# Four small moves in a one-core hybrid decoder layer: first weights on SyncE's queue, a decay subtraction on VectorE, a head's last transposes a step later, a last store in two

## The chip, the cores and the metric

The kernel runs on one core of a Trainium2 chip. The metric is device time in microseconds of one execution of the whole program. The engines are named as in the profile: PE is TensorE (matmuls), PEld its weight loads, DVE is VectorE, ACT is ScalarE, POOL is GpSimd and SP is SyncE, which here only issues DMAs. A letter q behind an engine's name means its own issuing of DMAs or semaphores.

## The reference

One decoder layer on 1024 tokens of width 1024, all in float32:

```python
h = rmsnorm(x, pre_g)
z = einsum('bsd,de->bse', h, w_in)       # one combined input projection
a_u, a_v, a_gate, b_q, b_k, b_v, b_gate, b_lr = split(z)
# branch A: gated unit over chunks of 128 tokens, 8 channel groups
a_out = chunked_sgu(gelu(a_u), gelu(a_v), ...) * silu(a_gate)
# branch B: gated linear attention, 4 heads, dk = 128, dv = 256, chunks of 64 tokens
log_a = log_sigmoid(b_lr @ w_a2 + b_a2) / 16
b     = cumsum(log_a, within a chunk)
qe, ke   = q * exp(b - b_ref), k * exp(b_ref - b)       # b_ref: b in the middle of the chunk
o_intra  = causal(qe @ ke.T) @ v
chunk_kv = (k * exp(b_last - b)).T @ v                  # b_last: b at the chunk's end
o_inter  = (q * exp(b)) @ state       # state = decay * state + chunk_kv, chunk by chunk
b_out = rmsnorm_per_head(o_intra + o_inter) * silu(b_gate)
y = concat(a_out, b_out) @ w_out                        # one output projection
out = x + rmsnorm(y, post_g)
```

Four exponentials are made of `b`: exp(b - b_ref), exp(b_ref - b), exp(b) and exp(b_last - b). The change touches the last one's argument.

## The kernel before

**Matmuls.** Every float32 matrix is held as a high part (a rounded copy that TensorE takes at full rate) and a low part (the rest). `split` (L108, L109) makes them: ScalarE casts the high part, VectorE (or GpSimd, where named) subtracts to get the low one. `mm3` (L114 to L116) then spends three matmuls on each product. A tile of 512 columns over the 1024 input channels is 8 times 3 = 24 matmuls.

**Start.** The 1024 tokens are 8 tiles of 128. `prep` (L267) takes one tile of x, computes its norm, scales it to `h` (L283, two halves) and transposes h on TensorE into `hT`, four transposes to a half, each half split into parts. The first tile's x comes in two halves on SyncE's queue (L263). `block_a` (L128) loads the weights of a block of 512 columns in four pieces of 256 channels, each piece as two DMAs of 256 KB (L135), and splits them into `gr`. In the first block (pieces `raw_125` to `raw_128` in the lists below) the first piece goes out on ScalarE's queue and the others on SyncE's. `first_block` (L209) multiplies a token tile with this block.

**The heads.** For each of four heads `gates` (L394) is run for each half of the tokens: it forms the logarithm of the decay (ScalarE: Abs, Exp, Ln), m (L408, L413), the running sum b by a scan (L415), `d` = b - b_ref (L420, VectorE) and `f` = b_last - b (L424, GpSimd), and the four exponentials on ScalarE: ke (L428), d (L429), b (L430), f (L431). ScalarE loads a table ahead of Exp after another function. `qk` (L441) multiplies them with the projections of q and k (ke L448, ks L449 to L451, d L454, m and b L455 to L457). For heads 2 and 3 the first half's gates are run ahead, during the head before. `attend` (L480) does one token tile: scores times values, the state `st` (L499), and the sums of squares and products of `og` (L513, L516). Every second token tile, GpSimd makes the reciprocal root and VectorE scales `og` (L520). These rows are transposed on TensorE (L527), copied by ScalarE (L528), and after four tiles written to DRAM as `mix_d` by a DMA of GpSimd (L534).

**What sets the order.** A small list of work for later: `later(fn, n)` (L75) puts a function down, and `tick()` (L78), which is called after every 12 matmuls of a projection, runs those that have come due at their n-th tick. So n says how many pieces of projection stand between. Beside this, a scheduler orders the instructions of each engine by its own model, unless `tc.issue_after` binds one behind another; so an edit in one place can move instructions of others. `gr` has 4 buffers, the raw weights 3, PSUM 8 banks.

**Beside the heads** sixteen units (L217 to L240) load blocks of the output weights, form four sums on VectorE (L230, 128x256 each), split them and store them; their DMAs are on SyncE's queue.

**After the heads** come the values and gates of branch A (L574 to L799): Gelu (L656), sums of hT (L609, L613) and their parts, statistics. Then the output projection, as seven products of blocks (`product`, L895). The last product's `done` (L979) squares and sums a token tile's result, and `finish` (L937) makes the root on GpSimd, scales and adds the residual (L942) and stores (L946), in the pieces it is given, on SyncE's and ScalarE's queue in turn. C0 and C1 are the first and the second 512 columns.

Of the kernel before, what the change touches and what calls it, by code (L numbers as in the profile page):

```python
# [11 lines left out]
AF = mybir.ActivationFunctionType  # L12
ALU = mybir.AluOpType
PSUM = bass.MemoryType.PSUM

P = 128
S = 1024
D = 1024
NT = S // P
# [5 lines left out]
CH = 64  # L25
TAU = 16.0
# [7 lines left out]
def hybrid_layer(  # L34
# [16 lines left out]
    nc = tc.nc  # L51
    x, out = x[0], out[0]
# [22 lines left out]
    def later(fn, n=1):  # L75
        pending.append([n, fn])
# [41 lines left out]
    W = 512  # L118
# [9 lines left out]
    def block_a(cols, raws=None, issued=None, behind={}):  # L128

        got = []  # L130
        for k2 in range(KT // 2):
            raw = raws[k2] if raws else raw_tile([2, W])
            c = 0
            for c0, n in cols:
                load = (nc.scalar if raws and k2 == 0 else nc.sync).dma_start(  # L135
                    raw[:, :, c : c + n],
                    w_in[k2 * 256 : (k2 + 1) * 256, c0 : c0 + n].rearrange("(k p) c -> p k c", p=P),
                )
                if issued is not None:
                    issued.append(load)  # L140
                c += n
            hi, lo = granule([2, W])
            if raws:
                for j in range(2):
                    with ExitStack() as order:
                        for made in behind.get(k2, ()):
                            order.enter_context(tc.issue_after(made.ins))
                        split(hi[:, j], lo[:, j], raw[:, j])
            else:
                split(hi, lo, raw)  # L150
            got += [(hi[:, j], lo[:, j]) for j in range(2)]
        return got
# [181 lines left out]
    with tc.tile_pool(name="gla", bufs=1) as gp:  # L334
# [3 lines left out]
            out=causal, in_=causal, pattern=[[1, P]], base=0, channel_multiplier=-1,  # L338
# [11 lines left out]
        for i in range(4):  # L350
# [4 lines left out]
            out=w2[32:64], in0=w2_raw[32:64], in1=w2[32:64].bitcast(F32), op=ALU.subtract  # L355
# [8 lines left out]
        for r, w in enumerate(w_lr):  # L364
            nc.gpsimd.memset(w.bitcast(F32), 0.0)
            src = lr_raw[:, 4 * r : 4 * r + 4]
            for i in (0, 1, 3):
                nc.scalar.copy(out=w[:, :, 32 * i : 32 * i + RANK], in_=src)
            nc.gpsimd.tensor_tensor(
                out=w[:, :, 64 : 64 + RANK], in0=src, in1=w[:, :, 0:RANK].bitcast(F32), op=ALU.subtract  # L370
# [23 lines left out]
        def gates(hd, hf):  # L394

            pz = bank()
            nc.tensor.matmul(
                pz, w2[:, hd * DK : (hd + 1) * DK], lrT[:, hf * 512 : (hf + 1) * 512],
                start=True, stop=True,
            )  # L400
            bias = ba[:, hd : hd + 1]

            f = gp.tile([P, 8, CH], F32, tag="f", name="f")
            sp = f.rearrange("p n c -> p (n c)")
            nc.scalar.activation(out=sp, in_=pz, func=AF.Abs, bias=bias)
            m = gp.tile([P, 8, CH], F32, tag="m", name="m")
            mf = m.rearrange("p n c -> p (n c)")
            nc.vector.tensor_scalar(  # L408
                out=mf, in0=pz, scalar1=bias, scalar2=0.0, op0=ALU.add, op1=ALU.min
            )  # L410
            nc.scalar.activation(out=sp, in_=sp, func=AF.Exp, scale=-1.0)
            nc.scalar.activation(out=sp, in_=sp, func=AF.Ln, bias=1.0)
            tt(out=mf, in0=mf, in1=sp, op=ALU.subtract)  # L413
            b = gp.tile([P, 8, CH], F32, tag="b", name="b")
            nc.vector.tensor_tensor_scan(  # L415
                out=b.rearrange("p n c -> p (n c)"), data0=seg, data1=mf, initial=0.0,
                op0=ALU.mult, op1=ALU.add,
            )
            d = gp.tile([P, 8, CH], F32, tag="d", name="d")
            tt(  # L420
                out=d, in0=b, in1=b[:, :, CH // 2 - 1 : CH // 2].to_broadcast([P, 8, CH]),
                op=ALU.subtract,
            )
            nc.gpsimd.tensor_tensor(  # L424
                out=f, in0=b[:, :, CH - 1 : CH].to_broadcast([P, 8, CH]), in1=b, op=ALU.subtract
            )
            ke = gp.tile([P, 8, CH], F32, tag="ke", name="ke")
            nc.scalar.activation(out=ke, in_=d, func=AF.Exp, scale=-1.0 / TAU)  # L428
            nc.scalar.activation(out=d, in_=d, func=AF.Exp, scale=1.0 / TAU)  # L429
            nc.scalar.activation(out=b, in_=b, func=AF.Exp, scale=1.0 / TAU)  # L430
            nc.scalar.activation(out=f, in_=f, func=AF.Exp, scale=1.0 / TAU)  # L431
            dec = gp.tile([P, LINE, 1], F32, tag="dec", name="dec", bufs=2)[:, 0:8]
            nc.vector.tensor_copy(dec, b[:, :, CH - 1 : CH])
            dec2 = gp.tile([P, LINE, 1], F32, tag="dec2", name="dec2", bufs=3)[:, 0:4]
            tt(out=dec2, in0=dec[:, 0::2], in1=dec[:, 1::2], op=ALU.mult)
            return b, d, f, ke, dec, dec2, m
# [48 lines left out]
        def attend(hd, t, got, v, sg, cur):  # L485
# [31 lines left out]
            if e == 1:  # L517
                rsqrt(oss, oss)
                for i in range(2):
                    nc.vector.tensor_scalar_mul(og[:, i], og[:, i], oss[:, i : i + 1])  # L520

                def out(t=t, og=og, mx=cur["mx"], hd=hd):
                    pt = bank()
                    ptv = pt.rearrange("p (e t c) -> p e t c", t=2, e=2)
                    for i in range(2):
                        for k in range(2):
                            nc.tensor.transpose(ptv[:, k, i], og[:, i, k * P : (k + 1) * P], ident)  # L527
                    nc.scalar.copy(  # L528
                        out=mx[:, :, (t - 1) * P : (t + 1) * P],
                        in_=pt.rearrange("p (e n) -> p e n", e=2),  # L530
                    )
                    if t % 4 == 3:
                        c = slice((t - 3) * P, (t + 1) * P)
                        nc.gpsimd.dma_start(  # L534
                            mix_d[2 * hd : 2 * hd + 2, :, c].rearrange("e p c -> p e c"), mx[:, :, c]
                        )

                later(out, 4 if t == NT - 1 else 3)

        def new_mix():  # L540
            return {"mx": slot_b([P, 2, S])}
# [273 lines left out]
    with tc.tile_pool(name="outp", bufs=1, side="right", reuse_waits="tile") as op:  # L815
# [121 lines left out]
        def finish(hf, t, xr, pieces):  # L937
            r = slice((4 * hf + t) * P, (4 * hf + t + 1) * P)
            rstd = small[:, 16 + 4 * hf + t : 17 + 4 * hf + t]
            rsqrt(rstd, ss[hf][t][:, 0:1], ss[hf][t][:, 1:2])  # L940
            for i, c in enumerate(pieces):
                nc.vector.scalar_tensor_tensor(  # L942
                    out=y[hf][t][:, c], in0=y[hf][t][:, c], scalar=rstd, in1=xr[:, c],
                    op0=ALU.mult, op1=ALU.add,
                )
                (nc.sync, nc.scalar)[i % 2].dma_start(out[r, c], y[hf][t][:, c])  # L946
# [32 lines left out]
        def done(t):  # L979
            sum_sq(ss[1][t][:, 0:1], u[t])  # L980
            vtt(out=y[1][t][:, C0], in0=u[t], in1=pog[:, C0], op=ALU.mult)
            finish(1, t, xrs[t], (C1, C0))

        product(u, "a22", "-t4", False, done)

# [24 lines left out]
```

## Time and profile before

| what | value |
|---|---|
| time, median of 3 runs | 776.02 us (773.84 to 777.74) |
| the profiled execution | 775.63 us |
| its span, first to last instruction | 773.9 us |
| TensorE busy | 753.5 us, 97% |
| VectorE busy | 499.8 us, 65% |
| ScalarE busy | 389.3 us, 50% |
| GpSimd busy | 131.2 us, 17% |
| mean granted TensorE clock | 0.999 |

The profile is of one execution. Busy time is the union of an engine's instructions, not a sign that it sets the time; the waits and the idle time in brackets, with what ended it, tell who was late. TensorE's instructions overlap, so a matmul's own duration is longer than the distance from one start to the next.

### The profile page before, as it was taken

Reading aid. Unit: us, or ns where it says so; the run is one execution under the profiler, and the core shown is the slowest. Engines: PE = TensorE matmul, PEld = TensorE weight load, DVE = VectorE, ACT = ScalarE, POOL = GpSimd, SP = SyncE. Lnnn points to the kernel's source line nnn. Section 1 sums busy time; section 2 is a strip of 40 time slices with the busy share of each in tenths; the row PEclk is TensorE's granted clock in tenths of the full one; section 3 lists DMA queues with packets and bytes.
Section 4 is the critical chain, followed back from the end, with each engine's and each line's share of the span. In section 5 each row is a group of like instructions: output and inputs, shape, how many; then the busy total and the mean of one; then the engine's idle time right before and its main releaser. Section 6 shows DMA issues by size and latency. Waiting matters only on the chain.

```text
span 773.9 us, 10106 instructions
## 1 busy us (share of the span) xinstructions
PE 753.5 (97%) x3680; PEld 622.8 (80%) x3680; DVE 499.8 (65%) x865; ACT 389.3 (50%) x680; POOL 131.2 (17%) x173
## 2 busy tenths in 40 slices
PE   6999999999999999999999999999999999999996
PEld 3787788787888888888878888888888788888885
DVE  4756689856666575654897289565565587534665
ACT  5635567637364746434442237556655652434431
POOL 2225144422222222322100000000000100000043
PEclk9999999999999999999999999999999999999999
DMA  9545520243622462343121012111211696346157
GB/s 293 182 135 177 170 76 1 83 177 121 199 82 83 154 220 72 107 162 112 57 80 28 0 55 55 55 54 55 55 54 55 206 356 226 109 164 244 56 217 272
DMA packets 79412, 97.87 MB, mean 126 GB/s; under 512 B 5569, under 2 KB 62913, under 8 KB 79362
## 3 DMA queue, kind: packets, MB, share of 16 engines
q1 hardware_dynamic: 75760, 87.64, 34.4%
q0 software_dynamic: 2480, 8.01, 3.3%
q10 hardware_dynamic: 1122, 1.58, 0.6%
q8 instruction: 29, 0.48, 0.3%
q14 instruction: 21, 0.17, 0.1%
HBM read 72.04 MB, written 25.17 MB: 126 GB/s over the span
## 4 chain that ended last, share of the span: by engine, by line
PE 74%; DVE 8%; DMA 6%; ACT 6%; issue 2%; POOL 1%; SPq 1%; DVEq 0%; POOLq 0%; ACTq 0%
PE ps L114 24%; PE ps L116 24%; PE ps L115 23%; DMA wb<-in_w_out_dram 3%; DMA wo_d<-wb 3%; PE ps L702 2%; DVE wb L230 1%; DVE wb L109 1%; DMA raw<-in_w_in_dram 1%; POOL f L424 1%; SPq L227 1%; ACT wh L108 1%; PE ps L527 1%; DVE og L520 1%; DVE stl L109 1%
## 5 line engine op out<-in xcount | busy, mean ns | idle before, releaser
L114 PE MATMUL ps<-gr,hT 128*128 128x512 f32 x384 | 152.3, 399 | 5.0 <-ACT hT L108 3.9
L116 PE MATMUL ps<-gr,hT 128*128 128x512 f32 x384 | 150.4, 393 | 0.0
L115 PE MATMUL ps<-gr,hT 128*128 128x512 f32 x384 | 150.2, 393 | 0.0
L109 DVE TENSOR_TENSOR gr<-raw,gr 128x1024 fp32r<-128x1024 f32 (+1 forms) x97 | 91.2, 961 | 22.9 <-ACT gr L108 22.3
L114 PE MATMUL ps<-hT,gr 128*128 128x512 f32 x256 | 100.3, 394 | 0.7 <-ACT u L775 0.7
L115 PE MATMUL ps<-hT,gr 128*128 128x512 f32 x256 | 100.0, 391 | 0.0
L116 PE MATMUL ps<-hT,gr 128*128 128x512 f32 x256 | 99.1, 393 | 0.0
L108 ACT CAST gr<-raw 128x1024 fp32r<-128x1024 f32 (+1 forms) x97 | 78.9, 838 | 36.8 <-PE ps L116 18.3
L114 PEld LDWEIGHTS ps<-gr,hT 128*128 128x128 f32 x384 | 72.8, 190 | 20.3 <-ACT hT L108 4.5
L116 PEld LDWEIGHTS ps<-gr,hT 128*128 128x128 f32 x384 | 72.7, 189 | 15.5 <-DVE hT L109 0.9
L114 PE MATMUL ps<-gr,ah 128*128 128x512 f32 x216 | 84.0, 389 | 0.0
L115 PE MATMUL ps<-gr,ah 128*128 128x512 f32 x216 | 84.0, 389 | 0.0
L115 PEld LDWEIGHTS ps<-gr,hT 128*128 128x128 f32 x384 | 72.8, 190 | 13.8
L116 PE MATMUL ps<-gr,al 128*128 128x512 f32 x216 | 81.4, 389 | 0.0
L114 PEld LDWEIGHTS ps<-hT,gr 128*128 128x128 f32 x256 | 48.1, 188 | 10.3 <-ACT u L775 1.2
L116 PEld LDWEIGHTS ps<-hT,gr 128*128 128x128 f32 x256 | 48.1, 188 | 10.2 <-DVE gr L109 0.2
L115 PEld LDWEIGHTS ps<-hT,gr 128*128 128x128 f32 x256 | 48.1, 188 | 9.6
L230 DVE TENSOR_TENSOR wb<-wb 128x256 f32<-128x256 f32 x64 | 28.8, 450 | 39.7 <-DMA wb<-in_w_out_dram 38.9
L115 PEld LDWEIGHTS ps<-gr,ah 128*128 128x128 f32 x216 | 40.5, 188 | 8.5
L114 PEld LDWEIGHTS ps<-gr,ah 128*128 128x128 f32 x216 | 40.5, 188 | 8.5
L116 PEld LDWEIGHTS ps<-gr,al 128*128 128x128 f32 x216 | 40.5, 188 | 8.3
L108 ACT CAST ah<-a 128x512 fp32r<-128x512 f32 x38 | 23.3, 622 | 46.7 <-PE ps L115 44.9
(232 smaller groups left out, 1323.5 us busy)
## 6 DMA issues: line engine op xcount, KB each, us to landing
raw<-in_w_in_dram SPq DMA_DIRECT2D x78, 256.0 KB, 3.2
gr<-wo_d SPq DMA_DIRECT2D x16, 1024.0 KB, 4.8
wb<-in_w_out_dram SPq DMA_DIRECT2D x64, 128.0 KB, 2.5
wo_d<-wh SPq DMA_DIRECT2D x16, 512.0 KB, 2.8
wo_d<-wb SPq DMA_DIRECT2D x16, 512.0 KB, 2.9
raw<-in_w_out_dram SPq DMA_DIRECT2D x12, 512.0 KB, 3.9
mix_d<-mixB POOLq DMA_DIRECT2D x8, 512.0 KB, 3.1
raw<-in_w_in_dram SPq DMA_DIRECT2D x8, 512.0 KB, 3.7
```

What stands on the lines that cost most here:

```text
L108: cast = nc.scalar.copy(out=hi, in_=src)
L109: return cast, (eng or nc.vector).tensor_tensor(out=lo, in0=src, in1=hi.bitcast(F32), op=ALU.subtract)
L114: nc.tensor.matmul(ps, a[0], b[0], start=start, stop=False, **how)
L115: nc.tensor.matmul(ps, a[0], b[1], start=False, stop=False, **how)
L116: nc.tensor.matmul(ps, a[1], b[0], start=False, stop=stop, **how)
L227: nc.sync.dma_start(b[:, i], w_out[(row + j) * P : (row + j + 1) * P, c : c + 256])
L230: sub = lambda out, a, c: nc.vector.tensor_tensor(out=out, in0=a, in1=c, op=ALU.subtract)
L424: nc.gpsimd.tensor_tensor(out=f, in0=b[:, :, CH - 1 : CH].to_broadcast([P, 8, CH]), in1=b, op=ALU.subtract)
L520: nc.vector.tensor_scalar_mul(og[:, i], og[:, i], oss[:, i : i + 1])
L527: nc.tensor.transpose(ptv[:, k, i], og[:, i, k * P : (k + 1) * P], ident)
L702: nc.tensor.matmul(pt[:, c], part[:, c], wsT[:, g], start=True, stop=True)
```

## The change

Four edits. The first block's first piece of weights is loaded by SyncE like the others. The subtraction `f` is made by VectorE, and the exponentials are written as ke first, and f, d and b bound to stand behind it. The transposes of a head's last two token tiles come due at the fifth tick and not at the fourth; the others stay at the third. The last piece of the last token tile (its first 512 columns) is scaled and stored as two pieces of 256.

```diff
--- before.py
+++ after.py
@@ -132,7 +132,7 @@
             raw = raws[k2] if raws else raw_tile([2, W])
             c = 0
             for c0, n in cols:
-                load = (nc.scalar if raws and k2 == 0 else nc.sync).dma_start(
+                load = nc.sync.dma_start(
                     raw[:, :, c : c + n],
                     w_in[k2 * 256 : (k2 + 1) * 256, c0 : c0 + n].rearrange("(k p) c -> p k c", p=P),
                 )
@@ -421,14 +421,13 @@
                 out=d, in0=b, in1=b[:, :, CH // 2 - 1 : CH // 2].to_broadcast([P, 8, CH]),
                 op=ALU.subtract,
             )
-            nc.gpsimd.tensor_tensor(
-                out=f, in0=b[:, :, CH - 1 : CH].to_broadcast([P, 8, CH]), in1=b, op=ALU.subtract
-            )
+            tt(out=f, in0=b[:, :, CH - 1 : CH].to_broadcast([P, 8, CH]), in1=b, op=ALU.subtract)
             ke = gp.tile([P, 8, CH], F32, tag="ke", name="ke")
-            nc.scalar.activation(out=ke, in_=d, func=AF.Exp, scale=-1.0 / TAU)
-            nc.scalar.activation(out=d, in_=d, func=AF.Exp, scale=1.0 / TAU)
-            nc.scalar.activation(out=b, in_=b, func=AF.Exp, scale=1.0 / TAU)
-            nc.scalar.activation(out=f, in_=f, func=AF.Exp, scale=1.0 / TAU)
+            first = nc.scalar.activation(out=ke, in_=d, func=AF.Exp, scale=-1.0 / TAU)
+            with tc.issue_after(first.ins):
+                nc.scalar.activation(out=f, in_=f, func=AF.Exp, scale=1.0 / TAU)
+                nc.scalar.activation(out=d, in_=d, func=AF.Exp, scale=1.0 / TAU)
+                nc.scalar.activation(out=b, in_=b, func=AF.Exp, scale=1.0 / TAU)
             dec = gp.tile([P, LINE, 1], F32, tag="dec", name="dec", bufs=2)[:, 0:8]
             nc.vector.tensor_copy(dec, b[:, :, CH - 1 : CH])
             dec2 = gp.tile([P, LINE, 1], F32, tag="dec2", name="dec2", bufs=3)[:, 0:4]
@@ -535,7 +534,7 @@
                             mix_d[2 * hd : 2 * hd + 2, :, c].rearrange("e p c -> p e c"), mx[:, :, c]
                         )
 
-                later(out, 4 if t == NT - 1 else 3)
+                later(out, 5 if t == NT - 1 else 3)
 
         def new_mix():
             return {"mx": slot_b([P, 2, S])}
@@ -979,7 +978,7 @@
         def done(t):
             sum_sq(ss[1][t][:, 0:1], u[t])
             vtt(out=y[1][t][:, C0], in0=u[t], in1=pog[:, C0], op=ALU.mult)
-            finish(1, t, xrs[t], (C1, C0))
+            finish(1, t, xrs[t], (C1, C0) if t < 3 else (C1, slice(0, W // 2), slice(W // 2, W)))
 
         product(u, "a22", "-t4", False, done)
```

(`t == NT - 1` is the last token tile of a head. In the lists of the changed kernel the lines behind 424 are one less than before: L520 becomes L519, L528 becomes L527, and so on; the exponentials stand at L426 ke, L428 f, L429 d, L430 b.)

VectorE at the start of the program, before. `raw_125` to `raw_128` are the first block's weights, `h` the normed first token tile:

```order
L283 SCALAR_TENSOR_TENSOR h<-xt,ss,ps 128x512 x2
L109 TENSOR_TENSOR gr<-raw_125,gr 128x512 x2
L109 TENSOR_TENSOR hT<-ps,hT 128x4x128
L109 TENSOR_TENSOR gr<-raw_126,gr 128x512 x2
L109 TENSOR_TENSOR hT<-ps,hT 128x4x128
```

And after:

```order
L283 SCALAR_TENSOR_TENSOR h<-xt,ss,ps 128x512
L109 TENSOR_TENSOR gr<-raw_125,gr 128x512 x2
L283 SCALAR_TENSOR_TENSOR h<-xt,ss,ps 128x512
L109 TENSOR_TENSOR hT<-ps,hT 128x4x128
L109 TENSOR_TENSOR gr<-raw_126,gr 128x512 x2
L109 TENSOR_TENSOR hT<-ps,hT 128x4x128
```

The second half of h moved behind the low parts of the first weights.

ScalarE in the second gates of head 1, before. L412 is the logarithm, `gr` are weights, `mixB` the copy of transposed rows:

```order
L412 ACTIVATE f<-f 128x512
L108 CAST gr<-raw 128x1024
L108 CAST sth<-st 128x256
L513 ACTIVATE og,oss<-ps 128x256
L528 COPY mixB<-ps 128x2x256
L431 ACT_TABLE_LOAD
L431 ACTIVATE f<-f 128x512
L428 ACTIVATE ke<-d 128x512
L430 ACTIVATE b<-b 128x512
L108 CAST gr<-raw 128x1024
L429 ACTIVATE d<-d 128x512
```

And after:

```order
L412 ACTIVATE f<-f 128x512
L108 CAST sch<-scm 128x512
L108 CAST gr<-raw 128x1024
L108 CAST sth<-st 128x256
L512 ACTIVATE og,oss<-ps 128x256
L527 COPY mixB<-ps 128x2x256
L108 CAST gr<-raw 128x1024
L426 ACT_TABLE_LOAD
L426 ACTIVATE ke<-d 128x512
L428 ACTIVATE f<-f 128x512
L430 ACTIVATE b<-b 128x512
L429 ACTIVATE d<-d 128x512
```

The second cast of weights moved ahead of the table load and the exponentials; f's exponential moved from the first to the second place.

VectorE in head 1, where the first gates of head 2 are run ahead, before. `m` (L408) is the first instruction of these gates on VectorE, `wb` are sums of output weights:

```order
L408 TENSOR_SCALAR m<-ps,ba 128x512
L499 SCALAR_TENSOR_TENSOR st<-st,dec_949,ps 128x256
L230 TENSOR_TENSOR wb<-wb 128x256
L413 TENSOR_TENSOR m<-m,f 128x512
L230 TENSOR_TENSOR wb<-wb 128x256
L516 TENSOR_TENSOR og<-ps,sg 128x256
L109 TENSOR_TENSOR stl<-st,sth 128x256
L415 SCALAR_TENSOR_TENSOR b<-seg,m 128x512
L230 TENSOR_TENSOR wb<-wb 128x256
L520 TENSOR_SCALAR og<-og,oss 128x256 x2
L499 SCALAR_TENSOR_TENSOR st<-st,dec_1161,ps 128x256
L420 TENSOR_TENSOR d<-b 128x512
```

And after:

```order
L515 TENSOR_TENSOR og<-ps,sg 128x256
L109 TENSOR_TENSOR stl<-st,sth 128x256
L109 TENSOR_TENSOR vl<-ps,vh 128x256
L519 TENSOR_SCALAR og<-og,oss 128x256 x2
L408 TENSOR_SCALAR m<-ps,ba 128x512
L230 TENSOR_TENSOR wb<-wb 128x256
L413 TENSOR_TENSOR m<-m,f 128x512
L230 TENSOR_TENSOR wb<-wb 128x256
L415 SCALAR_TENSOR_TENSOR b<-seg,m 128x512
L230 TENSOR_TENSOR wb<-wb 128x256
L420 TENSOR_TENSOR d<-b 128x512
L424 TENSOR_TENSOR f<-b 128x512
```

The two scalings of `og` moved ahead of the gates' first instruction, one update of the state ahead of this stretch, and f's subtraction (L424) is new behind d's.

## Rows read from the trace of the kernel before

**Rows 1.** The page: TensorE's busy us (share), instructions; granted clock by slice.

```profile
PE 753.5 (97%) x3680; PEld 622.8 (80%) x3680; DVE 499.8 (65%) x865; ACT 389.3 (50%) x680; POOL 131.2 (17%) x173
PEclk9999999999999999999999999999999999999999
```

**Rows 2.** TensorE's waits and what for: us in total, times, longest.

```profile
PE ps L114 <- ACT hT L108: 3.9, 2, 3.6
PE ps L527 <- DVE og L520: 1.8, 1, 1.8
PE ps L114 <- ACT gr L108: 1.1, 1, 1.1
PE ps L466 <- DVE d L454: 0.8, 1, 0.8
PE ps L114 <- ACT vh L108: 0.5, 1, 0.5
PE ps L468 <- DVE b L456: 0.4, 1, 0.4
```

**Rows 3.** Timeline, first 13 us: start, us, engine, line, operation [idle before].

```profile
1.35 0.42 ACTq L135 DMA_DIRECT2D raw<-in_w_in_dram  x1
3.45 0.38 ACTq L135 DMA_DIRECT2D raw<-in_w_in_dram  x1
6.39 1.41 DVE L283 SCALAR_TENSOR_TENSOR h<-xt,ss,ps 128x512 f32<-128x512 f32 x2 [5.31 <-POOL ss L103]
7.20 1.97 PE L290 MATMUL ps<-ident,h 128*128 128x128 f32 x8 [1.00 <-DVE h L283]
11.14 1.14 ACT L108 CAST gr<-raw 128x512 fp32r<-128x512 f32 x2 [5.84 <-DMA raw<-in_w_in_dram]
12.81 0.80 PE L114 MATMUL ps<-gr,hT 128*128 128x512 f32 x1 [3.65 <-ACT hT L108]
```

**Rows 4.** DMA issues at 1.35 and 3.45: KB, us to landing.

```profile
raw<-in_w_in_dram ACTq DMA_DIRECT2D x1, 256.0 KB, 4.8
raw<-in_w_in_dram ACTq DMA_DIRECT2D x1, 256.0 KB, 7.6
```

**Rows 5.** A stretch: busy (x) of five engines, clock, DMA share, GB/s.

```profile
10.00:11.00 1.00, 0.00 (x0) 0.00 (x0) 0.00 (x0) 0.00 (x0) 0.00 (x0) 1.00 1.12 355
```

**Rows 6.** Lines 424 and 420: ns min/median/max; who waited (us, times).

```profile
L424 POOL TENSOR_TENSOR f<-b x8: 1043/1746/2785, 82.4 to 303.2; 128x512 f32<-128x512 f32 x8
...
  ACT f L431: 9.1, 5
...
L420 DVE TENSOR_TENSOR d<-b x8: 679/1034/1529, 82.3 to 304.1; 128x512 f32<-128x512 f32 x8
```

**Rows 7.** Timeline of ScalarE and GpSimd, second gates of head 1.

```profile
137.95 2.79 POOL L424 TENSOR_TENSOR f<-b 128x512 f32<-128x512 f32 x1 [3.31 <-ACT mixB L528]
137.95 1.28 ACT L431 ACT_TABLE_LOAD   x1
142.34 1.03 ACT L108 CAST gr<-raw 128x1024 fp32r<-128x1024 f32 x1
```

**Rows 8.** Timeline of VectorE, first gates of head 2, within head 1.

```profile
180.43 1.40 DVE L520 TENSOR_SCALAR og<-og,oss 128x256 f32<-128x256 f32 x2
```

**Rows 9.** Timeline of VectorE and ScalarE after the last head.

```profile
370.75 2.50 DVE L609 TENSOR_TENSOR u<-hT 128x512 f32<-128x512 f32 x4 [5.69 <-PE ps L527]
377.55 1.28 ACT L656 ACT_TABLE_LOAD   x1 [0.51 <-DMA mix_d<-mixB]
408.22 1.21 DVE L109 TENSOR_TENSOR gr<-raw,gr 128x1024 fp32r<-128x1024 f32 x1
```

**Rows 10.** The end: timeline, a DMA issue, and 128x256 steps (busy, mean ns).

```profile
769.44 1.41 DVE L942 SCALAR_TENSOR_TENSOR y<-y,small,xr 128x512 f32<-128x512 f32 x2 [0.36 <-POOL small L103]
...
out_dram<-y ACTq DMA_DIRECT2D x2, 256.0 KB, 2.0
...
L230 DVE TENSOR_TENSOR wb<-wb 128x256 f32<-128x256 f32 x64 | 28.8, 450 | 39.7 <-DMA wb<-in_w_out_dram 38.9
```

## The prediction

> **What bounds the kernel now.** I read the page's busy times and slices first: TensorE is busy 753.5 of the span's 773.9 us, at a granted clock of 9 tenths or more in every slice [rows 1]. So the time is TensorE's instruction list plus its pauses, some 20 us, and an edit pays only where TensorE waits. The second view is TensorE's waits by what ended them [rows 2]: they are short and each has its own place. The largest, 3.9 us for hT, is nearly all at the start. Then come 1.8 us for `og` (the rows that a head's transposes read), 1.1 us for a cast `gr` (weights), 0.8 us for `d`, 0.5 for `vh`, 0.4 for `b`. The change can win only part of this, so the scale is a few microseconds, under 1%. I then looked at each place in the timeline, and last at the tail.
>
> **First weights.** Before, the first block's first two loads (256 KB each) go out on ScalarE's queue, at 1.35 and 3.45 us. They take 4.8 and 7.6 us to land [rows 4], so the first is there at 6.1 and the second at 11.05. ScalarE's casts wait 5.84 us for the latter and start at 11.14; hT's cast stands behind them, and the first matmul starts at 12.81 after 3.65 us of idleness [rows 3]. In that stretch the DMA engines are full (share 1.12 at 355 GB/s [rows 5]), so moving a load to another queue moves no byte faster; it changes whose bytes come first. After the change the two loads stand directly behind the two halves of x on SyncE, ahead of six loads that used to go in parallel. Landing T has the bounds 6.1 (where the first one was) and 11.05 (where the second was). I take T = 7.9: both loads one behind the other take 1.5 us at 355 GB/s, which put behind the 6.1 gives 7.6, and 0.3 for x, which shares the stretch.
> The order also changes on VectorE: the second half of h now stands behind both lo parts of these weights. From T on: two casts 1.14 us, the second lo 0.7 behind them (a subtraction of this shape takes 0.68 [rows 6]), half of h 0.7 (1.41 for two), four of the eight transposes about 1.0 (1.97 for eight) [rows 3], and some 0.2 of handing over: T + 3.7 = 11.6 for the first matmul, against 12.81: -1.2. At T = 7.0 the gain is 2.1; at 9.1 it is gone; at 11.05 it is a loss of 1.9; T = 6.1 would give 3.0. The first block's 24 matmuls then run as before.
> The second load's 7.6 us for 256 KB, 35 GB/s, is about a tenth of what the engines moved at 355 [rows 4, 5]. The Trainium skill ("DMA: Bandwidth & Descriptors", "Queues, rings and completion order") says that each DMA engine goes round the queues that have work, a packet at a time. By that, ScalarE's queue would have had half of the rate beside SyncE's alone, its second load would have been there before 8, and leaving its queue would win nothing: this term 0, the sum -2.15. The trace's tenth does not agree with a half, so I keep -1.2.
>
> **The decays' subtraction.** Eight instructions `f` leave GpSimd (median 1.75 us, 1.04 to 2.79) and become 128x512 subtractions on VectorE, like L420, whose fastest is 0.68: 8 x 0.69 = 5.5 us more work. Against it, L420 itself takes 1.03 in the median and 1.53 at worst, beside GpSimd's `f`; all eight at the fastest give back about 8 x (1.03 - 0.68) = 2.8. VectorE's net is under 3 us over 220 us in which it is far from full. ScalarE no longer waits 9.1 us for `f` [rows 6], and `ke` comes first of the four exponentials. What that is worth, place by place:
> Head 1's second gates. ScalarE loaded the table at 137.95, waited for GpSimd's 2.79 us `f`, and the cast `gr`, queued behind f, ke and b, started at 142.34 [rows 7]; TensorE stood 1.1 us for it [rows 2]. In the new order this cast stands ahead of the table load. At 142.34 it has no wait of its own, so no row shows its weights late; it would be done by 139.2, some 4 us early: -1.1. If something else is late there, 0.
> Head 2's first gates, run ahead within head 1. The scalings `og` stood on VectorE behind the scan and all that the scan waits for, at 180.43 [rows 8]; TensorE's transposes waited 1.8 [rows 2]. In the new order they stand ahead of the gate's first instruction: -1.8. Late next is `vh`, whose cast on ScalarE now stands behind ke, f, b and d together; where head 3's gates, run ahead in head 2, make such a queue, TensorE waits 0.5 for it [rows 2], so +0.5 here. Net -1.3 (bounds -1.8 and 0). That 0.5 itself loses GpSimd's part of its delay: -0.3 (-0.5 to 0).
> Cost: in the gates that a head runs for itself, `b` was the second exponential and is now the third or fourth, one exponential (0.63 or a little less) later, and the ks products come ahead of it on VectorE. Its product already is the last to come at one place, 0.4 us [rows 2]; there b slips by up to 1.2 while waits for ks go: +0.4 (0 to +1.2). The 0.8 for `d` stays. Elsewhere the cover is TensorE's projection matmuls, which do not need the decays; were it gone everywhere, rival D.
>
> **A head's last transposes.** `later` 5 instead of 4 sets them one projection piece, 12 matmuls, later: at 753.5 / 3680 = 0.2 us each [rows 1] about 2.5 us. TensorE does the same work, and none of its waits is there; in the first three heads only the copy and the DMA to `mix_d` stand behind them, which is read after the heads, so nothing. After the last head this moves: VectorE waited 5.69 us for these transposes and began its sums at 370.75, and ScalarE's table for GELU waited for the mix DMA until 377.55 [rows 9]. Both go 2.5 later. VectorE then works almost without a pause to the lo part at 408.22 [rows 9], which makes weights that TensorE takes soon after: little room. The new order has three 128x512 steps fewer ahead of that part, 1.9 us at 2.50 / 4 each. What passes through is 0 to 1.0; I take +0.3.
>
> **Last piece of the last token tile.** Two 128x512 steps (1.41 together) from 769.44 and a DMA of 2.0 us end the span. A 128x256 form takes 0.45 [rows 10], so two are 0.2 longer than one of 0.7, but the first goes out 0.25 earlier and both DMAs carry half the bytes, worth up to 0.4 of the 2.0: -0.15 (-0.35 to +0.3).
>
> **Sum.** -1.2 - 1.1 - 1.3 - 0.3 + 0.4 + 0.3 - 0.15 = -3.35. The profiled execution took 775.63 (span 773.9 and 1.7 around it), so 772.3; from the runs' median, 776.02, it is 772.7. I take 772.5.
>
> **Rivals.** 0.5% is 3.9 us, about what a measurement of this kernel can tell from no change: faster means under 772.1, slower over 779.9.
> A, the forecast: chance 0.48. Its own range is 770.9 to 774.0; 0.22 of it lies under 772.1.
> B, the start gains nothing: the engines are full there, T is 9 or later. For it: the share of 1.12 [rows 5], and that h now waits behind the lo parts. Against: the tenth of the rate that the second load had. -3.35 + 1.2 = -2.15: 773.6 from the point I took, 773 to 775.5 with T up to 11.05; chance 0.24, all of it the same.
> C, more is won: T = 7.0 (0.9 more), no new wait for vh (0.5) and b's product in time (0.4): -5.15, 770.7, or 769.6 with T = 6.1 and the edit at the last head free. For it: ScalarE is rid of 9.1 us of waits. Against: its queue then has four exponentials in a row. Chance 0.20, all faster.
> D, VectorE becomes the bound of the gates: `f` (0.69) stands in line ahead of the products, and f's exponential (0.5) ahead of b and d: 1.2 for each of eight gates, 9.6 us where nothing hides it. -3.35 + 9.6 = +6.25: 782. It makes the kernel slower from three gates of the eight (3.35 / 1.2) and passes the 0.5% from about six. For it: b's product is the last to come at one place. Against: TensorE's waits for d and b are 1.2 us together now [rows 2]. Chance 0.08, half of it over 779.9.
> The chances: faster 0.22 + 0.20 = 0.42, same 0.26 + 0.24 + 0.04 = 0.54, slower 0.04. The range goes from C's far end, 769.6, to 776.0, just over B's, and leaves out D and a little of C.
>
> **What would show it.** The first matmul near 11.6 and ScalarE's first cast near 7.9; the waits for `gr` L108 and `og` gone from TensorE's list; L420's eight all near 0.69; a new wait for `vh` near 183 and one for `b` near 126 of 0.4 to 1.6; the sums of the last stage's start 2.5 later and nothing new on TensorE from 370 to 412. It is wrong if the first cast still waits beyond 9, if waits for ke, ks or b appear in several gates, or if TensorE waits for lo parts of `gr` near 410.

## The result and the profile after

The changed kernel takes 770.10 us (median of 4 runs, 768.47 to 770.72) against 775.65 us of the kernel before (4 runs, 773.84 to 777.74): a ratio of 0.9937, with a 95% interval from 0.9919 to 0.9955, or 5.5 us less. Its profiled execution took 769.79 us, with a span of 768.1 us; the span of before was 773.9, so the two traces differ by 5.8 us. Each of them is of one execution. One execution of the experiments below, the traced one of the first edit alone, took 1950.67 us with its matmuls 0.62 us apart, and no number below is taken from it.

TensorE's waits in the changed kernel (what waited, for what, total, times, longest, in us):

```profile
PE ps L290 <- DVE h L283: 4.0, 2, 3.3
...
PE ps L114 <- ACT hT L108: 0.8, 1, 0.8
...
PE ps L475 <- DVE ks L450: 0.7, 1, 0.7
...
PE ps L526 <- DVE og L519: 0.3, 1, 0.3
PE ps L114 <- ACT vh L108: 0.2, 1, 0.2
```

Against [rows 2], the wait for `gr` L108 (1.1) is gone, that for `og` is 0.3 instead of 1.8 (and at the next pair of tiles, near 190; at the old place there is none), that for `vh` 0.2 instead of 0.5, and those for `d` (0.8) and `b` (0.4) are gone too; a wait for `ks` of 0.7 is new. At the start the wait has only changed its name: 3.3 us for `h` where 3.6 stood for hT.

Compared matmul by matmul, TensorE in the changed kernel is ahead of the kernel before by 1.0 us near 39 us, 2.5 near 112, 3.6 near 151, 5.1 near 200 and 6.0 near 312, and by 5.9 from 360 us on. These are the places of the start, of the pause for `d` and `b`, of the one for `gr`, of the one for `og`, and of several small ones.

The start, in the timeline of the changed kernel (start, us, engine, line, operation):

```profile
1.70 5.42 SPq L135 DMA_DIRECT2D raw<-in_w_in_dram  x8
...
8.57 1.14 ACT L108 CAST gr<-raw 128x512 fp32r<-128x512 f32 x2 [3.61 <-DMA raw<-in_w_in_dram]
9.22 1.29 DVE L109 TENSOR_TENSOR gr<-raw,gr 128x512 fp32r<-128x512 f32 x2 [2.42 <-ACT gr L108]
...
10.43 0.74 DVE L283 SCALAR_TENSOR_TENSOR h<-xt,ss,ps 128x512 f32<-128x512 f32 x1
...
11.23 1.11 PE L290 MATMUL ps<-ident,h 128*128 128x128 f32 x4 [3.25 <-DVE h L283]
...
11.99 0.77 PE L114 MATMUL ps<-gr,hT 128*128 128x512 f32 x1
```

The casts start at 8.57 instead of 11.14 [rows 3], 2.6 us earlier, but the first matmul at 11.99 instead of 12.81, only 0.8 earlier: between them stand the two lo parts, then the half of h (10.43), then its four transposes (11.23), as the new order on VectorE has it. The start differs from execution to execution, so one pair of traces is thin evidence. Over the experiments below, the first casts start between 8.57 and 9.41 in the four traces with the first edit and no other change at the start, and between 10.71 and 11.62 in the five without it; the 24th matmul of the first block starts between 19.00 and 19.57, against 19.75 to 20.82.

Lines 420 and 424 in the changed kernel (ns min/median/max), and the scalings of `og` (L519, before L520):

```profile
L420 DVE TENSOR_TENSOR d<-b x8: 678/682/692, 81.3 to 298.3; 128x512 f32<-128x512 f32 x8
...
L424 DVE TENSOR_TENSOR f<-b x8: 676/684/686, 81.9 to 298.9; 128x512 f32<-128x512 f32 x8
...
L519 DVE TENSOR_SCALAR og<-og,oss x32: 341/349/355, 111.5 to 358.8; 128x256 f32<-128x256 f32 x32
```

All eight of L420 take 0.68 now; its median was 1.03 and its worst 1.53 [rows 6]. No scaling takes more than 0.36; before, the two at 180.43 took 1.40 [rows 8].

The second gates of head 1 on ScalarE, in the changed kernel:

```profile
134.30 1.05 ACT L108 CAST gr<-raw 128x1024 fp32r<-128x1024 f32 x1
135.37 1.28 ACT L426 ACT_TABLE_LOAD   x1
137.06 0.63 ACT L426 ACTIVATE ke<-d 128x512 f32<-128x512 f32 x1 [0.40 <-DVE d L420]
```

The cast `gr` is ahead of the table load, where [rows 7] had it 4.4 us behind; ke waits 0.40 for `d` and nothing waits for `f`.

After the last head, VectorE and, by its waits from 360 to 410 us, TensorE (for which that view lists nothing):

```profile
367.61 2.50 DVE L608 TENSOR_TENSOR u<-hT 128x512 f32<-128x512 f32 x4 [8.41 <-PE ps L526]
...
402.88 1.22 DVE L109 TENSOR_TENSOR gr<-raw,gr 128x1024 fp32r<-128x1024 f32 x1
```

The sums start 3.1 us earlier than before [rows 9], in a stretch in which everything else is 5.9 earlier, so 2.7 later: 12 matmuls, 0.23 us apart, as the third edit should have it. TensorE does not notice.

### The profile page after: what moved, and what is told of

It is laid out like the page before. It is cut to its first block, busy times and chain, and to the rows that moved or that the text cites. A ratio compares the mean times of both kernels' runs of the same rounds, so it can differ in the third digit from the quotient of the medians.

```text
span 768.1 us, 10129 instructions
## 1 busy us (share of the span) xinstructions
PE 751.9 (98%) x3680; PEld 622.6 (81%) x3680; DVE 497.9 (65%) x874; ACT 390.0 (51%) x680; POOL 118.8 (15%) x165
## 4 chain that ended last, share of the span: by engine, by line
PE 84%; DMA 4%; ACT 4%; DVE 4%; issue 2%; POOL 1%; SPq 1%; POOLq 0%; DVEq 0%; ACTq 0%
PE ps L114 26%; PE ps L115 26%; PE ps L116 26%; DMA wo_d<-wb 2%; PE ps L701 2%; DMA wb<-in_w_out_dram 2%; PE ps L381 1%; DMA raw<-in_w_in_dram 1%; DVE wb L230 1%; PE ps L475 1%; PE ps L526 1%; DVE wb L109 1%; ACT wh L108 1%; PE ps L465 0%; PE ps L467 0%
## 5 line engine op out<-in xcount | busy, mean ns | idle before, releaser
L108 ACT CAST gr<-raw 128x1024 fp32r<-128x1024 f32 (+1 forms) x97 | 78.8, 838 | 36.1 <-PE ps L116 19.3
L108 ACT CAST ah<-a 128x512 fp32r<-128x512 f32 x38 | 23.3, 622 | 46.7 <-PE ps L115 42.8
```

What stands on the lines that cost most here:

```text
L108: cast = nc.scalar.copy(out=hi, in_=src)
```

## The experiments

All were timed beside the kernel before on the same chip; there were three chips. Ratios are to that kernel, with 95% intervals; each is estimated from the single runs and need not equal the quotient of the two medians.

| kernel | median us | before, same chip | ratio (interval) |
|---|---|---|---|
| first edit alone | 773.68 | 774.44 | 0.9990 (0.9978 to 1.0001) |
| second edit alone | 771.25 | 774.44 | 0.9960 (0.9945 to 0.9974) |
| f on VectorE, order not bound | 770.35 | 774.44 | 0.9949 (0.9934 to 0.9964) |
| order bound, f on GpSimd | 773.51 | 774.44 | 0.9985 (0.9977 to 0.9993) |
| third and fourth edit alone | 775.40 | 773.91 | 1.0014 (1.0005 to 1.0023) |
| all four, again | 769.78 | 774.53 | 0.9937 (0.9923 to 0.9951) |
| all but the third | 771.13 | 773.91 | 0.9952 (0.9938 to 0.9966) |
| all, order not bound | 768.75 | 774.53 | 0.9924 (0.9909 to 0.9938) |
| all, h and hT first | 769.95 | 774.53 | 0.9939 (0.9921 to 0.9957) |
| all, the norm's gain later | 767.31 | 774.53 | 0.9906 (0.9891 to 0.9921) |
| gain later, order not bound | 766.57 | 773.91 | 0.9892 (0.9879 to 0.9906) |
| the same, h and hT first | 769.06 | 773.91 | 0.9928 (0.9914 to 0.9941) |

**First edit alone.**

```diff
-                load = (nc.scalar if raws and k2 == 0 else nc.sync).dma_start(
+                load = nc.sync.dma_start(
```

> The kernel before with the first edit alone (first block's first weights on SyncE's queue). Theory 1, each place pays for itself: first matmul near 12.0 us instead of 12.81, the time 0.8 to 1.0 us under the kernel before's, and TensorE's pauses at 93 (1.6 us), 143 (1.3) and 182 (1.9) unchanged. Theory 2, the earlier start also moves the later loads past each other: the pause at 93 goes too, together 2.2 to 2.6 us. Theory 3, the start gains nothing because what follows catches up: within 0.3 us.

Measured: 0.76 us under the kernel before, at the edge of what the runs can tell. That is the first theory's size. The second's 2.2 us is outside the interval (1.7 us at most); the third (within 0.3) is not, since the interval includes no change. What speaks for a gain are the starts of the first block in the other traces, given above.

**Second edit alone.** The kernel before with the diff's parts in `gates`.

> The kernel before with the second edit alone (f on VectorE and the new order of exponentials). Theory 1: first matmul still at 12.8, the pauses at 143, 182 and 268 shrink by 1.3, 1.5 and 0.4, a new one of 0.9 near 125, so 3.0 to 3.5 us less; if the pause at 93 goes as well (it went in the changed kernel), 4.5. Rival: the gates' gain needs the other edits' order, under 1.5 us.

Measured: 3.2 us less. TensorE's waits have none for `gr` L108, 0.2 for `vh`, a new 0.7 for ks, none for `d` and `b`. But `og` is still waited for:

```profile
PE ps L526 <- DVE og L519: 1.0, 1, 1.0
```

and on VectorE the scalings stand at the old place, behind the scan, only shorter:

```profile
176.23 1.22 DVE L415 TENSOR_TENSOR_SCAN b<-seg,m 128x512 f32<-128x512 f32 x1
...
177.68 0.61 DVE L519 TENSOR_SCALAR og<-og,oss 128x256 f32<-128x256 f32 x2
```

So 0.8 of that wait's 1.8 is the second edit's (two scalings in 0.61 where 1.40 was taken beside GpSimd's `f`), and the rest is not.

**Which half of the second edit.** One kernel has f on VectorE with the exponentials written as before, one the new order with f on GpSimd.

```diff
 # f on VectorE only
-            nc.gpsimd.tensor_tensor(
-                out=f, in0=b[:, :, CH - 1 : CH].to_broadcast([P, 8, CH]), in1=b, op=ALU.subtract
-            )
+            tt(out=f, in0=b[:, :, CH - 1 : CH].to_broadcast([P, 8, CH]), in1=b, op=ALU.subtract)
 # order only
+            first = nc.scalar.activation(out=ke, in_=d, func=AF.Exp, scale=-1.0 / TAU)
+            with tc.issue_after(first.ins):
+                nc.scalar.activation(out=f, in_=f, func=AF.Exp, scale=1.0 / TAU)
...
```

> The kernel before with f on VectorE but the exponentials written and bound as before. Theory 1a, the engine makes the gain (no wait for GpSimd on ScalarE): as the run with both, 3 us or more less, since the scheduler then also has ke first. Rival 1b, the written order makes it: no more than 1 us less, with the pause at 143 still above 0.8.

> The kernel before with f left on GpSimd but ke bound to be first. Theory 1a, the engine makes the gain: ScalarE still waits for f (over 4 us in all), b's product is late in several gates, and the time is within 1 us of the kernel before. Rival 1b, the order makes it: the pause at 143 is gone because the cast of weights is ahead of the table load, and the time is 2.5 us or more less.

Measured: the engine alone gives 4.1 us, the order alone 0.9. The engine is the cause. My reason for it was half wrong, though: in the order-only kernel ScalarE hardly waits for GpSimd any more, since ke comes first,

```profile
L424 POOL TENSOR_TENSOR f<-b x8: 1041/1656/1870, 82.6 to 301.7; 128x512 f32<-128x512 f32 x8
...
  ACT f L430: 0.3, 1
```
```profile
PE ps L528 <- DVE og L521: 1.8, 1, 1.8
```

(0.3 against 9.1 in [rows 6]) and the cast `gr` is no longer late either; yet only 0.9 us comes of it, and TensorE still waits 1.8 for `og` and 0.5 for `vh`. With ScalarE's wait nearly gone, 2.3 of the second edit's 3.2 us are still to be had by moving `f` off GpSimd. So most of what GpSimd's subtraction costs here is not ScalarE's wait for its result. One part of it is seen: a scaling of `og` beside it takes 1.13 us instead of 0.35, and TensorE's wait for `og` is 1.8 instead of 1.0. Where the rest of the 2.3 goes is not shown place by place; that it is VectorE's other instructions beside `f` (L420 with up to 1.53 for 0.68) is the likely reading.

**All four again, and not bound.** The second has the exponentials written as before.

> The changed kernel once more, beside the others of this call, as their yardstick. Expected 4.0 to 5.5 us under the kernel before on this chip. If the pause near 92 us (1.6 us before, gone after) was only a late landing of one execution and no part of the change, this execution has it or has it not by chance, and the gain of the medians is nearer 4.0; if the change removes it, it stays gone.

> The changed kernel without the bound order: the exponentials written as before (ke, d, b, f), f still on VectorE. Theory: the bound order costs, since it puts f's exponential ahead of b's, so that b's product is later; 0.5 to 1.0 us under the changed kernel, and the pause of 0.9 near 125 shrinks. Rival: the bound order is what made the gain; 1 us or more over the changed kernel. If nothing depends on it: within 0.3.

Measured: 4.75 us less for the changed kernel on this chip, and 1.0 us less again without the bound order, as 0.9 between the two kernels of the second edit above. The order puts f's exponential ahead of b's. Without it TensorE's wait for ks (0.7) gives way to one for `stl` (0.5) at the same place, and a few smaller ones go; so both pairs point the same way, but the intervals of each pair overlap, and the gain is not shown beyond them.

**Third and fourth edit alone, and all but the third.**

```diff
-                later(out, 4 if t == NT - 1 else 3)
+                later(out, 5 if t == NT - 1 else 3)
...
-            finish(1, t, xrs[t], (C1, C0))
+            finish(1, t, xrs[t], (C1, C0) if t < 3 else (C1, slice(0, W // 2), slice(W // 2, W)))
```

> The kernel before with the third and the fourth edit alone (a head's last transposes at the fifth tick, the last piece in two). Theory, new since the prediction: the third edit is what sets the scalings of og ahead of head 2's first gates, so TensorE's pause of 1.9 us near 181 is gone although f is still on GpSimd; the pause of 1.3 at 143 stays; the time 1.5 to 2 us under the kernel before. Rival, as predicted: the second edit removed that pause, this kernel still has it and is 0.3 us slower to 0.2 faster. The end behind the last matmul: 0.15 shorter as predicted, or the same. And a second look at the pause near 93: 1.6 us again if it belongs to this order of the instructions, gone if it was one late landing.

> The changed kernel without the third edit. Theory: the scalings of og stand behind the scan again, but take 0.6 us and not 1.4 since no GpSimd subtraction runs beside them: a pause of 1.0 to 1.2 us near 177, the time 0.8 to 1.5 us over the changed kernel (769.8 in the call before). Rival, as predicted: without the third edit the time is the same or 0.3 us lower.

Measured: alone, these two edits make the kernel 1.5 us slower (1.1 by the ratio); in the changed kernel the third is worth some 1.2 us (the ratios 0.9952 and 0.9937, on two chips; their intervals overlap). My expectation for the first was wrong in its sign, and its waits show why:

```profile
PE ps L114 <- ACT vh L108: 1.7, 2, 1.0
PE ps L114 <- ACT gr L108: 1.1, 1, 1.1
PE ps L115 <- DVE stl L109: 1.1, 1, 1.1
...
PE ps L466 <- DVE d L454: 0.6, 1, 0.6
PE ps L468 <- DVE b L456: 0.4, 1, 0.4
```

The wait for `og` is gone, so it is the third edit that sets the scalings ahead of head 2's first gates. But `vh` (1.0 at one place, 0.7 at the other) and `stl` (1.1) are now late: the pause has moved to what stood behind it. Without the third edit, the changed kernel has the wait for `og` again, 1.0 us, and the scalings stand behind the scan (L415, at 175.96), as with the second edit alone:

```profile
177.41 0.61 DVE L519 TENSOR_SCALAR og<-og,oss 128x256 f32<-128x256 f32 x2
```

**The start.** One kernel puts h and the first half of hT ahead of the first weights' parts; one moves the first load of the norm's gain (the same 1 KB into each of 128 partitions) from GpSimd's queue at 1.34 us to SyncE's behind the token tiles.

```diff
 # h and hT first
-            {1: made[0], 2: made[1]},
+            {0: made[0] + made[1][2:], 1: made[1]},
 # gain later
-        nc.gpsimd.dma_start(bg0, row_bc(bn_g[0:DV], DV))
+        with behind():
+            issued.append(nc.sync.dma_start(bg0, row_bc(bn_g[0:DV], DV)))
```

> The changed kernel with the first token tile's h and the first half of hT ahead of the first weights' parts on VectorE and ScalarE. Theory, the start is set by the order behind the landing T and not by T alone: first matmul at T + 0.9, near 9.4 instead of 12.0, the time 1.5 to 2.5 us under the changed kernel. Rival, the transfers bound the whole start: the first matmul is earlier but TensorE then waits for the later weights or for the second token tile, and the time is within 0.5 us.

> The changed kernel with the first 128 KB of the norm's gain, read once for all 128 partitions, issued by SyncE behind the second and third token tile and not by GpSimd at 1.3 us. Theory: this transfer is why only 88 to 153 GB/s flow from 4 to 6 us; the first weights then land at 7.0 to 7.5 instead of 8.5 and the time falls by 1.0 to 1.5 us. Rival, the start of any transfer is slow: landing within 0.3 of 8.5 and the time unchanged.

With h first, the first matmul comes at 9.23, 2.8 us earlier than in the changed kernel, and the time does not move (769.95 against 769.78 on the same chip): the rival. TensorE then waits for the third token tile's h, twice:

```profile
17.42 1.04 PE L290 MATMUL ps<-ident,h 128*128 128x128 f32 x8
19.66 0.66 PE L290 MATMUL ps<-ident,h 128*128 128x128 f32 x4 [1.20 <-DVE h L283]
21.68 1.09 PE L290 MATMUL ps<-ident,h 128*128 128x128 f32 x4 [1.37 <-DVE h L283]
```

From 19 to 21 us TensorE is busy a third of the time, and then its granted clock falls to 0.50, the lower of its two levels, for 3.4 us (the last three numbers are clock, DMA share and GB/s):

```profile
20.00:21.00 1.00, 0.31 (x3) 0.07 (x1) 0.81 (x2) 1.00 (x3) 0.48 (x1) 1.00 1.02 356
21.00:22.00 1.00, 0.32 (x2) 0.35 (x3) 1.00 (x2) 1.00 (x3) 0.22 (x1) 0.63 0.93 352
22.00:23.00 1.00, 1.00 (x6) 0.90 (x5) 0.46 (x2) 0.35 (x2) 0.57 (x1) 0.50 1.02 348
```

The six runs of this kernel agree with that as far as six can: three have a mean granted clock of 0.996, the traced one among them, and take 769.98 to 772.23; the other three have 0.998 or 0.999 and take 768.02 to 769.91.

An earlier first matmul can also be worth less than it seems. In every trace used here the first matmuls of the first block stand 0.43 us apart and the later ones 0.23. For 512 columns these are the paces of the lower and the higher of TensorE's two clock levels (1.2 and 2.4 GHz), though the view's clock column shows 1.00 already. With h first 11 matmuls go at the slow pace; in the changed kernel it is 11 in one trace and 6 in the other, each 0.2 us longer. So the 24th matmul starts at 17.18, only 1.8 us ahead of the changed kernel's 19.00 on the same chip, where the first was 3.2 ahead (9.23 against 12.41).

With the gain later the time falls by 2.5 us more (767.31 against 769.78, on the same chip), beyond the 1.0 to 1.5 that I expected. The windows from 4 to 6 us, first of the changed kernel and then with the gain later:

```profile
4.00:5.00 1.00, 1.00 (x2) 0.33 (x1) 0.00 (x0) 0.95 (x4) 0.00 (x0) 1.00 0.81 88
5.00:6.00 1.00, 1.00 (x2) 0.00 (x0) 0.00 (x0) 0.00 (x0) 0.85 (x2) 1.00 0.84 153
```
```profile
4.00:5.00 1.00, 1.00 (x3) 0.33 (x1) 0.00 (x0) 0.88 (x4) 0.00 (x0) 1.00 0.96 297
5.00:6.00 1.00, 1.00 (x2) 0.00 (x0) 0.00 (x0) 0.08 (x1) 0.73 (x2) 1.00 1.00 323
```

The DMA engines were busy in both, but with this transfer among them they moved 88 and 153 GB/s and without it 297 and 323. By queue, from 4 to 6 us (packets, MB, share of 16 engines' time): the kernel before, the changed kernel, and the one with the gain later. q0 is GpSimd's queue, which holds the gain alone there, q1 SyncE's:

```profile
q0 software_dynamic: 32, 0.11, 49.1%
```
```profile
q0 software_dynamic: 31, 0.09, 47.4%
q1 hardware_dynamic: 156, 0.15, 34.7%
```
```profile
q1 hardware_dynamic: 638, 0.62, 97.7%
```

So the gain took nearly half of the engines' time for 0.1 MB, in the kernel before as well. The broadcast as such need not be slow. On GpSimd's queue the 128 KB go as 32 packets of 4 KB, and these take 0.6 us each in the median here. Of the later reads of the gain on that queue in the kernel before, the next one, near 78 us, is as slow (0.57), and the last two, near 206 and 288, take 0.16 a packet. On SyncE's queue the read moved goes as 128 packets of 1 KB near 13 us, at 0.046 us each in the median, like the packets of the weights; it takes 8 us of the engines' time in all, and 19 before. The edit changes the queue, the packets and the time together; which of them cures it is open. The same read from SyncE's queue at 1.3 us would tell more and was not run.

The first weights' casts and the first matmul follow:

```profile
6.78 1.14 ACT L108 CAST gr<-raw 128x512 fp32r<-128x512 f32 x2 [1.70 <-DMA raw<-in_w_in_dram]
```
```profile
10.21 0.78 PE L114 MATMUL ps<-gr,hT 128*128 128x512 f32 x1
```
```profile
11.21 0.63 PE L116 MATMUL ps<-gr,hT 128*128 128x512 f32 x1
...
16.14 0.39 PE L114 MATMUL ps<-gr,hT 128*128 128x512 f32 x1
```

Both are 1.8 us earlier than in the first trace of the changed kernel and 2.2 earlier than in its trace on this chip. There too the slow pace takes some of it back (12 matmuls against 6): the 24th matmul is 1.05 us ahead of that trace's. TensorE has no wait for the third token tile's h here, so the gain is not lost there; it waits 0.88 for hT. At the end these two traces differ by 0.8 us (spans 766.1 and 766.9), so most of the 2.5 between the medians is not seen in them.

**Together.** The gain later and the order not bound; then h first on top.

> The changed kernel with the gain's transfer on SyncE's queue (the last call's fastest) and the exponentials written as before, not bound. If the two gains add up: 767.3 - 1.0 = about 766.3, 8 us under the kernel before. If they are one and the same, or the order shifts elsewhere: 767 to 768.

> The same, and h with the first half of hT ahead of the first weights' parts. The first matmul then near 7.6 us. Theory from the run of that alone: the second and third token tile set the end of the start, so no more than 0.5 us comes of it, and a wait for h near 18 to 20 us with a lower granted clock behind it can cost as much: within 0.7 us of the run without. Rival: with the transfers earlier the token tiles are earlier too and most of the 2 us comes through, 764.5.

The first is the fastest kernel of all, 766.57 us, 7.3 us under the kernel before by the medians (1.1% by the ratio), and the two gains add up: 0.9906 for the gain later and 0.0013 for the order would make 0.9893, and it is 0.9892. With h first it is 2.5 us slower: worse than both theories had it. The first matmul comes at 9.02 and not near the 7.6 that I expected. The two traces differ by 1.2 us only (spans 765.0 and 763.8), so half of that is not seen in them, and the trace with h first is of its fastest run by 2 us. What is seen is the third token tile's h, late again by 0.79 and 1.77:

```profile
18.68 0.66 PE L290 MATMUL ps<-ident,h 128*128 128x128 f32 x4 [0.79 <-DVE h L283]
21.11 0.63 PE L290 MATMUL ps<-ident,h 128*128 128x128 f32 x4 [1.77 <-DVE h L283]
```

The granted clock does not fall behind these pauses in this trace. The other four runs of this kernel have a mean clock of 0.996 or 0.997, against 0.998 or 0.999 without h first, so a fall in them is possible; it is not shown.

## Why the prediction was right or wrong

The time, 770.1, lies inside the range and on the forecast's side of it; the likeliest case, 772.5, is 2.4 us too slow, and even its own range (770.9 to 774.0) ends above it. It came out at rival C's size, 770.7, and by two of C's three conditions: there was no new wait for `vh`, and b's product cost next to nothing. The third did not come, T was not 7.0. In its place 1.5 us came from a pause that the sum had as staying, the one for `d`. Without that one the time would still be inside the range. By the terms of the sum, with the traces of the two kernels:

- **The start, -1.2.** First matmul 0.8 earlier, TensorE 1.0 ahead behind the start, and the edit alone is 0.76 us. T was 8.6 (up to 9.4 in other traces) and not 7.9; the order behind it cost 3.4 to 3.5, near the 3.7 that I had counted. The step that failed is the reason for T: I took the DMA engines as full and asked only whose bytes come first. They were busy, at 88 and 153 GB/s for two microseconds, and nearly half of their time went to a transfer on GpSimd's queue that the argument did not look at. The trace of before has it too (216 and 150 GB/s). The tenth of the rate that I held against rival B was a misreading: 7.6 us is the time from the issue of ScalarE's second load to its landing, and its packets moved only from 7.7 to 10.5 us. Why they began 4 us behind the issue is open. In that stretch its queue, q10, moved a quarter of all bytes, not a tenth and not a half, so this trace is no evidence against the rule that I had set the tenth against. Rival B (nothing gained) is not what the traces show, though the first edit's own interval does not exclude it. By queue, from 7.7 to 10.5 us, before (packets, MB, share of 16 engines' time):

```profile
q1 hardware_dynamic: 800, 0.77, 82.5%
q10 hardware_dynamic: 271, 0.26, 27.3%
```

- **Head 1's second gates, -1.1.** Right, 1.3 in the traces: the wait for `gr` is gone there, in all traced kernels that have either half of the second edit.
- **Head 2's first gates, -1.8 + 0.5.** The size came out (-1.6: no pause where 1.8 was, 0.3 new for `og` at the next pair of tiles, and none for `vh`), the cause did not. I put the move of `og` down to the second edit; it is the third edit's. The second shortened the scalings, and took the waits for `vh` and `stl` away that the third makes alone. I had read this from the order of all four edits together and given it to the edit that is written next to it.
- **The third edit, +0.3.** Wrong by that: I said that it could do nothing in the first three heads. Its cost after the last head is nothing.
- **b's product, +0.4.** Some +0.2, and of ks instead of b. I had read the 0.4 for `b` in [rows 2] as the pause near 126; it stands at 93.55, behind the one for `d`. Near 126 there were 0.2 for `b` and 0.2 for `vh`, and 0.7 for ks took their place.
- **Head 3's gates, -0.3.** Right: 0.5 became 0.2.
- **The wait for `d`, "stays".** It went (0.8, and the following 0.4 for `b` with it). TensorE gains 1.5 us there. It hangs on the first sums of output weights on VectorE, which wait for a DMA. It was there in both traces with the gates of before (0.8 and 0.6), 0.4 us in the kernel without the third edit, and not in the ten others. The DMA landed 7.2 and 6.7 us after its issue in the first two, 4.9 to 6.1 in the rest. Why it lands later there was not settled; that some of it is scatter is likely, and the median gain of 4.75 on the second chip is smaller than the 5.8 between the two traces.
- **The last piece, -0.15.** Nothing: from the start of the last matmul to the end it is 6.71 to 6.78 us in nine traces with two pieces and 6.73 or 6.74 in four with one. The first of the two goes out earlier, but 128 KB lands no faster than the 256 of [rows 10]:

```profile
out_dram<-y ACTq DMA_DIRECT2D x1, 128.0 KB, 2.1
out_dram<-y SPq DMA_DIRECT2D x1, 128.0 KB, 2.0
```

Rival D (VectorE the bound of the gates) fell: the eight `f` take 0.68 each as expected, and no engine is seen waiting for them.

The alone-times do not add up: -0.8, -3.2 and +1.5 make -2.5, together it is -4.75. The second and third edit seem worth more together: the third alone runs into waits for `vh` and `stl` that are gone with the second, and the second alone keeps 1.0 of the wait for `og` that is gone with the third.

## What to carry to other kernels

Where a scheduler orders the instructions, give each move in the order to the edit that makes it, by looking at the order with one edit at a time, before giving it a price. A DMA share near 1 does not say that the engines move what they can: read GB/s beside it, and the share of each queue: here one load of 128 KB on GpSimd's queue held nearly half of the engines' time. The time from a DMA's issue to its landing is no measure of its rate. An earlier first matmul is not yet an earlier end: read where the same matmul stands 10 and 20 us later. An instruction of GpSimd that nobody waits for can still cost the instructions that VectorE runs beside it.

## What the runs showed of the hardware

One load of 128 KB on GpSimd's queue, beside SyncE's loads at the start, went with a DMA rate of 88 and 153 GB/s for two microseconds at a busy share of 0.81 to 0.84; without it the same two windows show 297 and 323. Its 4 KB packets took 0.6 us in the median; those of two such loads later in the program took 0.16, and so the length of a packet alone does not make it slow.

A two-input subtraction on VectorE and one on GpSimd do not run side by side here; one waits for the other, whole and not in part. In the kernel before, GpSimd's `f` and VectorE's L420 in the first and the second gates of head 0 (start, us):

```profile
82.39 1.47 POOL L424 TENSOR_TENSOR f<-b 128x512 f32<-128x512 f32 x1 [6.01 <-DVE b L415]
...
100.95 1.85 POOL L424 TENSOR_TENSOR f<-b 128x512 f32<-128x512 f32 x1 [2.73 <-DVE b L415]
```
```profile
82.27 0.69 DVE L420 TENSOR_TENSOR d<-b 128x512 f32<-128x512 f32 x1
...
101.82 1.53 DVE L420 TENSOR_TENSOR d<-b 128x512 f32<-128x512 f32 x1
```

Where L420 starts first, it takes its 0.69, and `f` takes 1.47 where its shortest is 1.04; where `f` is already running, L420 ends 0.55 after that one. The Trainium skill ("SBUF — State Buffer", "Who interferes with whom") says that the two engines share a pair of ports under an exclusive lock, and that a VectorE instruction with two inputs in SBUF contends with a GpSimd one that reads there; of VectorE's two-port modes it says that whoever issues first has the pair for the whole instruction. These four rows agree with the first two, and show of these subtractions what the third says of the two-port modes.

A store of 128 KB at the end takes the 2.0 us of one of 256 KB. TensorE's granted clock fell to 0.50 for 3.4 us behind pauses of 1.2 and 1.4 us, in a stretch where it was busy a third of the time; in another trace it did not fall behind pauses of 0.8 and 1.8 us in such a stretch.
